# 100 tokens instead of 96 gathered in a product-key expert layer: a third group of four, more gathers in the query, first residuals between the last sums of v

## The chip, the cores and the metric

The kernel runs on one core of one Trainium2 chip. The metric is the device time of one launch in microseconds. A core has TensorE (PE, matmul, with its weight loads shown apart as PEld), VectorE (DVE), ScalarE (ACT), GpSimd (POOL) and SyncE (SP, which here only issues DMAs). 16 DMA engines move the data.

## The reference

One decoder layer on 256 tokens of width 2048, all in float32: attention (eight differential heads, eight stick-breaking heads) and an output projection, then a product-key expert layer (PEER), then a gated embedding, with a layer norm behind each. The part that matters here is PEER, over 16384 experts, of which each token uses 8 heads x 16:

```
q = (xt @ wq).reshape(t, PEER_HEADS, PEER_QDIM)
sa, sb = scores of the two halves of q against 128 keys each
va, ia = lax.top_k(sa, PEER_TOPK)
vb, ib = lax.top_k(sb, PEER_TOPK)
top, sel = lax.top_k(va + vb over all pairs, PEER_TOPK)
eidx = ia * PEER_NKEYS + ib at sel
gates = jax.nn.softmax(top, axis=-1)
act = jax.nn.gelu(einsum('thed,td->the', u[eidx], x))
out = einsum('the,thed->td', gates * act, v[eidx])
```

Then `x = layer_norm(alpha * x + out)`.

## The kernel before

**Two ways through PEER.** Of the 256 tokens the first NSP = 96 are sparse and the other NDT = 160 dense. For the dense tokens all 16384 experts are computed. The first pass (u) has 128 blocks `ia` of 128 experts; a block (`u_block`) loads 1 MB of `peer_u`, multiplies it in 16 matmuls with the 160 columns of `XF`, and ACT writes the Gelu into `A`. f32 matmuls show as two instructions each, so there are 4096. `gate_work` then builds, from one-hot matrices, the gate of each (expert, token) pair (`ps_G`) and multiplies it into `A`, first during the second 64 blocks of u, then during the first 64 blocks of v. The second pass (v) runs twice over the 128 blocks, once for each half of the 2048 outputs, eight matmuls a block (`v_block`, `v_mm`; one load of 1 MB for two blocks).

For the sparse tokens the rows of `peer_u` and `peer_v` that they need are gathered. A group of n tokens (`GROUPS`) puts 128/n copies of its tokens on the 128 partitions, and each copy handles n of the token's 128 experts. So one gather (an indirect DMA on POOL into a tile `gb`, 128 rows of 8 KB, 1 MB) serves 128 pairs of token and expert, and a group of n needs n gathers for u and n for v: 192 in all. DVE uses each: in u (L794) it multiplies `gb` with `xq`, the tokens' rows, and sums; in v (L800) it adds `gb` times a weight `ew` to `y`. `sparse_out` sums the copies with a matmul against a selecting matrix.

**What sets the order.** A planner places the instructions of each engine in the order in which it expects them to be ready; those wrapped in `keep` stay in the order in which they are written. DVE, ACT and POOL work their queue in that order. The DMAs of the weights are issued by SP into five buffers of 1 MB (`wf`).

Gathers are paced: after each block, `gathers(n)` adds n to a running sum, and for each whole number reached one gather is written. It begins with a `mark`, a DMA of four bytes in SP's queue behind the weight loads; POOL copies it (`pace`), and only then issues the gather. So a gather is released when SP has got so far, about five loads ahead of PE. The paces are GQ = 1.3 a block in the query (from the fourth of 16 blocks on), GU = 0.715 in u, GV = 0.3575 in v. There are NGB = 3 buffers `gb` and 32 marks; gather k's use is written behind the issue of gather k+2.

**Top-k work.** The query's 16 blocks make the scores of the 8 heads. After every second one, `topk_work` does one head of the first 128 tokens on DVE and POOL (`topk_heads(0, h, 1)`, `head_slots`), and `place` writes the head's expert numbers into `eig` with small DMAs on POOL. In u each block runs one step: `gates(0)`, the softmax of the first 128 tokens, whose Exp (L702) stands in ACT's queue and waits for a subtraction on DVE (L700); then the 34 steps of `topk_heads(1, 0, 8)`; then `gates(1)` and the transposes for `gate_work`.

**The end of v.** The last STAG = 6 blocks of the second half are loaded ahead (`held`) and summed output by output, so that `v_out` can copy a finished pair of outputs to `yT` while PE sums the next. `res2` transposes `yT` back and adds the residual. `sparse_out` stands after block 113 of the second half, `res2` of the first half of the outputs after blocks 114 and 115, and two loads of `ple_gate` with their splitting (`sg2.parts`) after blocks 116 and 119.

Of the kernel before, what the change touches and what calls it, by code (L numbers as in the profile page):

```python
# [38 lines left out]
SEG1 = 64  # L39
SEG2 = NIA - SEG1  # L40

GROUPS = ((0, 64), (64, 32))
NSP = sum(n for _, n in GROUPS)
NDT = T - NSP
SELB = 8
NGB = 3

GQ = 1.3
GU = 0.715
GV = 0.3575  # L50
GSCALE = 2.0 ** 15
GB = 5
OHB = 5
# [102 lines left out]
def build(tc, a, out):  # L156
# [496 lines left out]
        yield from ()  # L653

    keep = tc.keep_in_program_order

    def topk_heads(t, h0, n):

# [38 lines left out]
    def gates(t):  # L697

        g = gate[:, t]
        keep(nc.vector.tensor_tensor(g, CV[:, t], CV[:, t, :, 0:1].to_broadcast([P, PH, TOPK]),  # L700
                                     op=ALU.subtract))
        keep(nc.scalar.activation(g, g, AF.Exp))  # L702
# [17 lines left out]
        place(0, slice(h, h + 1), 0)  # L720

    def place(i, hs, w):
        t0, n = GROUPS[i]
        m = n // PH
        dst = eig[i].rearrange("p w (h m) -> p w h m", h=PH)
        for q in range(P // n):
            nc.gpsimd.dma_start(dst[q * n:(q + 1) * n, w, hs],
                                eg[t0:t0 + n, w, hs, q * m:(q + 1) * m])

    def topk_work():  # L730
        nc.vector.tensor_copy(io128, io128f)
        for h in range(PH):
            for _ in topk_heads(0, h, 1):
                pass
            head_slots(h)
            yield
        for i in range(1, len(GROUPS)):
            place(i, slice(0, PH), 0)
# [31 lines left out]
    def sparse_work():  # L770

        xq = []
        for i, (t0, n) in enumerate(GROUPS):
            xq.append(gin.tile([P, D], F32, name=f"xq{i}", tag=f"xq{i}"))
            for q in range(P // n):
                nc.gpsimd.dma_start(xq[i][q * n:(q + 1) * n, :], a["s_x1"][t0:t0 + n, :])
        made = []

        dots, acts = [], []

        def advance():

            if acts:
                i, b = acts.pop(0)
                keep(nc.vector.tensor_tensor(ew[i][:, b], ew[i][:, b],
                                             eig[i][:, 1, b].bitcast(F32), op=ALU.mult))
            if dots:
                i, b = dots.pop(0)
                keep(nc.scalar.activation(ew[i][:, b], eact[i][:, b], AF.Gelu_apprx_tanh))
                acts.append((i, b))  # L790

        def use(kind, i, j, g):
            if kind == "u_rows":
                keep(nc.vector.scalar_tensor_tensor(g, g, 1.0, xq[i], op0=ALU.mult, op1=ALU.mult,  # L794
                                                    accum_out=eact[i][:, j:j + 1]))
            elif j == 0:
                ys[i] = gin.tile([P, D], F32, name=f"y{i}", tag=f"xq{i}")
                keep(nc.vector.tensor_scalar(ys[i], g, ew[i][:, j:j + 1], None, op0=ALU.mult))
            else:
                keep(nc.vector.scalar_tensor_tensor(ys[i], g, ew[i][:, j:j + 1], ys[i],  # L800
                                                    op0=ALU.mult, op1=ALU.add))
            if j % SELB == SELB - 1:
                advance()
                if kind == "u_rows":
                    dots.append((i, slice(j + 1 - SELB, j + 1)))

        for kind in ("u_rows", "v_rows"):
            for i, (_, n) in enumerate(GROUPS):
                for j in range(n):

                    mark = gin.tile([1, 1], F32, name="mark", tag="mark", bufs=32)
                    keep(nc.sync.dma_start(mark, a["c_iota"][0:1, 0:1]))
                    keep(nc.gpsimd.tensor_copy(pace, mark))  # L813
                    g = gin.tile([P, D], F32, name="gb", tag="gb", bufs=NGB)
                    keep(nc.gpsimd.indirect_dma_start(  # L815
                        out=g, out_offset=None, in_=a[kind],
                        in_offset=bass.IndirectOffsetOnAxis(ap=eig[i][:, 0, j:j + 1], axis=0)))
                    made.append((kind, i, j, g))
                    if len(made) >= NGB:
                        use(*made.pop(0))  # L820
                    yield
        while made:
            use(*made.pop(0))

    def sparse_out():

        for i, (t0, n) in enumerate(GROUPS):
            per = min(ND, 512 // n)
            for d0 in range(0, ND, per):
                ps = pbank(pp, "ps_y")  # L830
                for j in range(per):
                    keep(nc.tensor.matmul(ps[:, j * n:(j + 1) * n],  # L832
                                          ys[i][:, (d0 + j) * P:(d0 + j + 1) * P], sel[i],
                                          start=True, stop=True))
                nc.scalar.copy(yT[:, d0:d0 + per, t0:t0 + n],  # L835
                               ps[:, :per * n].rearrange("p (j t) -> p j t", j=per))
# [190 lines left out]
    for ia in range(SEG1, NIA - STAG):  # L1027
        v_block(1, ia, psv2, keep if ia >= NIA - STAG - 16 else lambda ins: ins)
        gathers(GV)
        if ia == NIA - STAG - 14:  # L1030
            while not run(sparse, 1):
                pass
        if ia == NIA - STAG - 9:
            sparse_out()
        if ia in (NIA - STAG - 8, NIA - STAG - 7):
            for t in range(NT):
                res2(t, 4 * (ia - NIA + STAG + 8), 4)
        if ia in (NIA - STAG - 6, NIA - STAG - 3):
            sg2.order = keep
            parts0 += list(sg2.parts(a["ple_gate"][0, len(parts0) // 4]))  # L1040
    held = [v_load(1, ia) for ia in range(NIA - STAG, NIA)]
# [224 lines left out]
```

## Time and profile before

| | |
|---|---|
| median of 3 runs | 1825.09 us (1825.09 to 1826.13) |
| profiled execution | 1826.57 us, its span 1824.6 us |
| PE busy | 1786.7 us, 98% |
| DVE busy | 1045.2 us, 57% |
| ACT busy | 544.4 us, 30% |
| POOL busy | 500.6 us, 27% |
| moved by DMA | 599.33 MB, mean 328 GB/s |
| mean granted TensorE clock | 0.995 |

The groups of the profile give a line of the kernel, an engine, an operation, the tile written and those read, the shapes, how often, the busy time in microseconds and the mean of one instruction in ns, then the idle time ahead of it and what ended that. Matmuls overlap, so busy time divided by count is their distance, and the mean of one is longer. A row of stretches has each engine's busy time with the count, then the granted clock, the share of the DMA engines and GB/s. In the timeline a row is a start, a duration and a run of like instructions. Some matmul records are missing. By stages: the query runs from 417 to 533 us, u to 1119, the first half of v to 1415, and the second to 1704.

### The profile page before, as it was taken

The numbers are of one execution on the slowest core, as the hardware profiler recorded it, in microseconds if no ns is written. First come the engines' busy times: TensorE is split into PE (matmuls) and PEld (weight loads), VectorE is DVE, ScalarE is ACT, GpSimd is POOL, SyncE is SP. The second block draws the span as 40 slices with busy tenths as digits, with TensorE's granted clock in tenths as the row PEclk, the third lists the DMA queues.
The fourth block names the chain that finished last, engine by engine and source line by source line (L and its number), as shares of the span: only waits on it lengthen the run. The fifth ranks groups of instructions, "written<-read, shape, count | busy, mean of one in ns | idle before, by whom it ended". The sixth has DMA issues, their size and how long they took to land.

```text
span 1824.6 us, 30303 instructions
## 1 busy us (share of the span) xinstructions
PE 1786.7 (98%) x12094; PEld 1679.9 (92%) x12094; DVE 1045.2 (57%) x1643; ACT 544.4 (30%) x1365; POOL 500.6 (27%) x579
## 2 busy tenths in 40 slices
PE   8999999999999999999999999999999999999896
PEld 6888888888899999999999999999999999999766
DVE  5555588654677894543554544975433333343686
ACT  5677477642010001002333331862000000001532
POOL 0133033006445242322222212222234233220241
PEclk9999999999999999999999999999999999999998
DMA  7554644668789999999999999999999999996561
GB/s 278 187 171 163 231 145 156 231 212 266 306 316 374 420 420 416 395 420 401 415 379 383 380 391 353 420 419 350 421 421 420 415 416 415 419 421 267 212 258 53
DMA packets 98717, 599.33 MB, mean 328 GB/s; under 512 B 13072, under 2 KB 14912, under 8 KB 35600
## 3 DMA queue, kind: packets, MB, share of 16 engines
q1 hardware_dynamic: 66768, 384.24, 54.4%
q0 software_dynamic: 30080, 208.57, 28.5%
q10 hardware_dynamic: 1728, 4.59, 0.7%
q8 instruction: 95, 1.56, 0.3%
q14 instruction: 46, 0.38, 0.1%
HBM read 590.96 MB, written 6.29 MB: 327 GB/s over the span
## 4 chain that ended last, share of the span: by engine, by line
PE 82%; issue 6%; DVE 5%; DMA 4%; POOL 2%; ACT 1%; SPq 0%; DVEq 0%; POOLq 0%; ACTq 0%
PE ps_v L956 30%; PE ps_u L206 23%; PE ps_qk L195 7%; PE ps_qk L197 3%; PE ps_q L206 2%; PE ps_v L214 2%; PE ps_v L215 2%; PE ps_v L213 2%; PE ps_mix L213 1%; PE ps_mix L214 1%; PE ps_mix L215 1%; DMA wf<-peer_u 1%; PE ps_gate L214 1%; PE ps_gate L213 1%; PE ps_gate L215 1%
## 5 line engine op out<-in xcount | busy, mean ns | idle before, releaser
L206 PE MATMUL ps_u<-XF,wf 128*128 128x160 f32 x4096 | 572.4, 301 | 6.8 <-ACT A L906 6.6
L956 PE MATMUL ps_v<-A,wf 128*128 128x160 f32 x4096 | 569.1, 301 | 0.6 <-DVE A L877 0.6
L206 PEld LDWEIGHTS ps_u<-XF,wf 128*128 128x128 f32 x4096 | 560.3, 191 | 9.7 <-ACT A L906 8.8
L956 PEld LDWEIGHTS ps_v<-A,wf 128*128 128x128 f32 x4096 | 558.5, 191 | 1.6 <-DVE A L877 0.7
L800 DVE SCALAR_TENSOR_TENSOR y<-gb,ew,y 128x2048 f32<-128x2048 f32 x94 | 220.9, 2350 | 242.0 <-DMA gb<-v_rows,eig 241.8
L108 DVE TENSOR_TENSOR wl<-wf,wh 128x1024 fp32r<-128x1024 f32 (+1 forms) x201 | 222.7, 1132 | 98.3 <-ACT wh L107 97.0
L794 DVE SCALAR_TENSOR_TENSOR gb<-gb,xq 128x2048 f32<-128x2048 f32 x96 | 218.7, 2286 | 93.3 <-DMA gb<-u_rows,eig 90.5
L107 ACT CAST wh<-wf 128x1024 fp32r<-128x1024 f32 (+1 forms) x201 | 172.8, 889 | 111.7 <-PE ps_qk L195 29.4
L815 POOL DMA_INDIRECT gb<-u_rows,eig x96 | 101.3, 1055 | 334.4 <-DVE gb L794 213.9
L195 PE MATMUL ps_qk<-X,wh 128*128 128x512 f32 x512 | 185.2, 401 | 0.0
L815 POOL DMA_INDIRECT gb<-v_rows,eig x96 | 115.8, 1206 | 196.8 <-DVE y L800 148.8
L906 ACT ACTIVATE A<-ps_u 128x160 f32<-128x160 f32 x128 | 38.5, 303 | 434.7 <-PE ps_u L206 389.4
L813 POOL COPY pace<-mark 1x1 f32<-1x1 f32 x192 | 95.3, 496 | 252.1 <-DMA mark<-c_iota 251.4
L197 PE MATMUL ps_qk<-X,wl 128*128 128x256 f32 x512 | 146.1, 285 | 0.0
L859 ACT ACTIVATE hi<-eq,ghf 128x64 f16<-128x64 f16 x320 | 107.3, 335 | 52.5 <-DVE eq L853 48.5
L195 PEld LDWEIGHTS ps_qk<-X,wh 128*128 128x128 f32 x512 | 96.6, 189 | 21.9 <-issue 1.0
L206 PE MATMUL ps_q<-XF,wf 128*128 128x256 f32 x512 | 113.5, 380 | 0.0
L853 DVE TENSOR_TENSOR eq<-io,iaT 128x320 f16<-128x320 f16 x64 | 31.2, 488 | 133.8 <-ACT lo L860 133.8
L206 PEld LDWEIGHTS ps_q<-XF,wf 128*128 128x128 f32 x512 | 96.2, 191 | 12.0
L860 ACT ACTIVATE lo<-eq,glf 128x64 f16<-128x64 f16 x320 | 107.0, 334 | 0.0
L197 PEld LDWEIGHTS ps_qk<-X,wl 128*128 128x128 f32 x512 | 96.4, 188 | 2.5 <-issue 1.3
L835 ACT COPY XF<-ps_y 128x512 f32<-128x512 f32 x3 | 1.8, 585 | 253.2 <-PE ps_y L832 253.2
(232 smaller groups left out, 1791.2 us busy)
## 6 DMA issues: line engine op xcount, KB each, us to landing
wf<-peer_u SPq DMA_DIRECT2D x128, 1024.0 KB
wf<-peer_v SPq DMA_DIRECT2D x128, 1024.0 KB
wf<-w_qk SPq DMA_DIRECT2D x64, 512.0 KB
wf<-w_out SPq DMA_DIRECT2D x32, 512.0 KB
wf<-peer_wq SPq DMA_DIRECT2D x16, 1024.0 KB
wf<-ple_gate SPq DMA_DIRECT2D x16, 1024.0 KB
wf<-w_v SPq DMA_DIRECT2D x31, 512.0 KB
mark<-c_iota SPq DMA_DIRECT2D x192, 0.0 KB
```

Of the source, the lines that this page charges most:

```text
L107: self.order(nc.scalar.copy(wh, src))
L108: self.order(nc.vector.tensor_tensor(wl, src, wh.bitcast(F32), op=ALU.subtract))
L195: nc.tensor.matmul(ps, wh[:, j * P:(j + 1) * P], xt[:, dt, :], start=dt == 0, stop=False)
L197: nc.tensor.matmul(ps[:, :T], wl[:, j * P:(j + 1) * P], xt[:, dt, :T], start=False, stop=dt == ND - 1)
L206: nc.tensor.matmul(ps[:, :T - t0], wf[:, dt * P:(dt + 1) * P], xt[:, dt, t0:], start=dt == 0, stop=dt == ND - 1)
L794: keep(nc.vector.scalar_tensor_tensor(g, g, 1.0, xq[i], op0=ALU.mult, op1=ALU.mult, accum_out=eact[i][:, j:j + 1]))
L800: keep(nc.vector.scalar_tensor_tensor(ys[i], g, ew[i][:, j:j + 1], ys[i], op0=ALU.mult, op1=ALU.add))
L813: keep(nc.gpsimd.tensor_copy(pace, mark))
L815: keep(nc.gpsimd.indirect_dma_start(out=g, out_offset=None, in_=a[kind], in_offset=bass.IndirectOffsetOnAxis(ap=eig[i][:, 0, j:j + 1], axi ...
L859: nc.scalar.mul(hi[:, j, :], eq[:, j, :], ghf[:, t])
L860: nc.scalar.mul(lo[:, j, :], eq[:, j, :], glf[:, t])
L956: return nc.tensor.matmul(ps[:, (j % 2) * NDT:(j % 2 + 1) * NDT], vf[:, j * P:(j + 1) * P], W_of(ia), start=False, stop=ia == NIA - 1 and ...
```

## The change

- A third group of four tokens: 100 are sparse and 156 dense. It needs four gathers for u and four for v, 200 in all. Its tokens stand on the partitions in 32 copies, so its part of `xq` comes in 32 DMAs of 32 KB on POOL, and `place` writes its expert numbers and gates in 32 small DMAs on SP instead of POOL, once both are known.
- Paces: GQ 2.0, GU 0.695, GV 0.3475. So 26 gathers are marked in the query, and v's last one after block 116 of the second half.
- `gates(0)` comes after five of the 16 selections of the second 128 tokens; after eight further steps follows the third group's `place`. The gates are multiplied into `ew` only once they are there (`gated`).
- `sparse_out` stands behind the last loads of v, directly ahead of the last sums; `res2` of the first outputs moves between the last sums; the loads of `ple_gate` come after blocks 113 and 117.

```
-GROUPS = ((0, 64), (64, 32))
+GROUPS = ((0, 64), (64, 32), (96, 4))
-GQ = 1.3
-GU = 0.715
-GV = 0.3575
+GQ = 2.0
+GU = 0.695
+GV = 0.3475
...
+    gated = []
...
-            for i in range(len(GROUPS)):
-                place(i, slice(0, PH), 1)
+            for i, (_, n) in enumerate(GROUPS):
+                if n >= PH:
+                    place(i, slice(0, PH), 1)
+            gated.append(t)
...
     def place(i, hs, w):
         t0, n = GROUPS[i]
+        if n < PH:
+            for q in range(P // n):
+                nc.sync.dma_start(eig[i][q * n:(q + 1) * n],
+                                  eg[t0:t0 + n, :, q // TOPK::PH // n, q % TOPK])
+            return
...
+        second = topk_heads(1, 0, PH)
+        for _ in range(5):
+            next(second)
+            yield
         yield from gates(0)
-        yield from topk_heads(1, 0, PH)
+        for _ in range(8):
+            next(second)
+            yield
+        for i, (_, n) in enumerate(GROUPS):
+            if n < PH:
+                place(i, slice(0, PH), slice(0, 2))
+        yield from second
         yield from gates(1)
...
-            if acts:
+            if acts and gated:
...
-            if j % SELB == SELB - 1:
+            if j % SELB == SELB - 1 or j == GROUPS[i][1] - 1:
                 advance()
                 if kind == "u_rows":
-                    dots.append((i, slice(j + 1 - SELB, j + 1)))
+                    dots.append((i, slice(j - j % SELB, j + 1)))
...
-        if ia == NIA - STAG - 14:
+        if ia in (NIA - STAG - 9, NIA - STAG - 5):
+            sg2.order = keep
+            parts0 += list(sg2.parts(a["ple_gate"][0, len(parts0) // 4]))
+        if ia == NIA - STAG - 3:
             while not run(sparse, 1):
                 pass
-        if ia == NIA - STAG - 9:
-            sparse_out()
-        if ia in (NIA - STAG - 8, NIA - STAG - 7):
-            for t in range(NT):
-                res2(t, 4 * (ia - NIA + STAG + 8), 4)
-        if ia in (NIA - STAG - 6, NIA - STAG - 3):
-            sg2.order = keep
-            parts0 += list(sg2.parts(a["ple_gate"][0, len(parts0) // 4]))
     held = [v_load(1, ia) for ia in range(NIA - STAG, NIA)]
-    for b in range(4):
+    sparse_out()
+
+    between = [(), ((0, 4),), (), ((4, 4), (8, 2)), (), ((10, 2),), (), ((12, 2),)]
+    for j in range(8):
+        for d0, nd in between[j]:
+            for t in range(NT):
+                res2(t, d0, nd)
         for ia in range(NIA - STAG, NIA):
-            for j in (2 * b, 2 * b + 1):
-                v_mm(psv2[b], j, ia, held[ia - NIA + STAG])
-        v_out(1, b, psv2[b])
-        if b < 3:
-            for t in range(NT):
-                res2(t, 8 + 2 * b, 2)
+            keep(v_mm(psv2[j // 2], j, ia, held[ia - NIA + STAG]))
+        if j % 2:
+            v_out(1, j // 2, psv2[j // 2])
```

More of the change, by code (lines that the diff above doesn't have):

```diff
@@ L737, in topk_work @@
         for i in range(1, len(GROUPS)):
-            place(i, slice(0, PH), 0)
-        yield from gates(0)
-        yield from topk_heads(1, 0, PH)
+            if GROUPS[i][1] >= PH:
+                place(i, slice(0, PH), 0)
+        second = topk_heads(1, 0, PH)
+        for _ in range(5):
+            next(second)
+            yield
+        yield from gates(0)
+        for _ in range(8):
[5 more added lines that the diff above has]
+        yield from second
         yield from gates(1)
@@ L1029, in build @@
         gathers(GV)
-        if ia == NIA - STAG - 14:
+        if ia in (NIA - STAG - 9, NIA - STAG - 5):
+            sg2.order = keep
+            parts0 += list(sg2.parts(a["ple_gate"][0, len(parts0) // 4]))
+        if ia == NIA - STAG - 3:
             while not run(sparse, 1):
                 pass
-        if ia == NIA - STAG - 9:
-            sparse_out()
-        if ia in (NIA - STAG - 8, NIA - STAG - 7):
-            for t in range(NT):
-                res2(t, 4 * (ia - NIA + STAG + 8), 4)
-        if ia in (NIA - STAG - 6, NIA - STAG - 3):
-            sg2.order = keep
-            parts0 += list(sg2.parts(a["ple_gate"][0, len(parts0) // 4]))
-    held = [v_load(1, ia) for ia in range(NIA - STAG, NIA)]
-    for b in range(4):
-        for ia in range(NIA - STAG, NIA):
-            for j in (2 * b, 2 * b + 1):
-                v_mm(psv2[b], j, ia, held[ia - NIA + STAG])
-        v_out(1, b, psv2[b])
-        if b < 3:
-            for t in range(NT):
-                res2(t, 8 + 2 * b, 2)
+    held = [v_load(1, ia) for ia in range(NIA - STAG, NIA)]
+    sparse_out()
+    between = [(), ((0, 4),), (), ((4, 4), (8, 2)), (), ((10, 2),), (), ((12, 2),)]
+    for j in range(8):
+        for d0, nd in between[j]:
+            for t in range(NT):
+                res2(t, d0, nd)
+        for ia in range(NIA - STAG, NIA):
+            keep(v_mm(psv2[j // 2], j, ia, held[ia - NIA + STAG]))
+        if j % 2:
+            v_out(1, j // 2, psv2[j // 2])
     stats2 = []
```

## The prediction

> **What bounds the kernel now.** I read first the page's busy times, then the groups by shape, then stretches of the span stage by stage, then the order of single instructions where PE stands.
>
> ```profile
> PE 1786.7 (98%) x12094; PEld 1679.9 (92%) x12094; DVE 1045.2 (57%) x1643; ACT 544.4 (30%) x1365; POOL 500.6 (27%) x579
> L206 PE MATMUL ps_u<-XF,wf 128*128 128x160 f32 x4096 | 572.4, 301 | 6.8 <-ACT A L906 6.6 <-DMA wf<-peer_u 0.2
> L956 PE MATMUL ps_v<-A,wf 128*128 128x160 f32 x4096 | 569.1, 301 | 0.6 <-DVE A L877 0.6
> ```
>
> PE is the bound: 98% busy, and 8192 of its instructions are the two dense passes over the experts, one column for each of the 160 dense tokens. Next, the stretches: the query, three parts of the first pass (u), the part in which the gate matrices are also built, and the second half of v.
>
> ```profile
> core 0: us, PE busy (x) PEld busy (x) DVE busy (x) ACT busy (x) POOL busy (x), PEclk, DMA share, GB/s
> 417.00:533.00 116.00, 116.00 (x570) 103.21 (x569) 72.43 (x236) 14.08 (x36) 60.76 (x71) 1.00 0.80 288
> 561.00:640.00 79.00, 75.83 (x544) 75.59 (x544) 63.61 (x183) 7.73 (x24) 26.13 (x43) 0.98 1.00 403
> 640.00:665.00 25.00, 23.05 (x161) 22.02 (x162) 24.17 (x64) 1.61 (x6) 4.57 (x8) 1.00 1.01 421
> 820.00:1270.00 450.00, 449.15 (x3724) 443.57 (x3725) 254.85 (x306) 175.07 (x712) 101.77 (x138) 1.00 0.97 390
> 1270.00:1640.00 370.00, 370.00 (x2721) 369.52 (x2720) 143.14 (x62) 1.70 (x4) 115.39 (x125) 1.00 1.01 417
> ```
>
> Transfers are the second bound, and close: 421 GB/s is the most any stretch shows, v runs at 417, and only the query (288) has room. Where transfers are full, PE can lose:
>
> ```profile
> 645.01 4.59 PE L206 MATMUL ps_u<-XF,wf 128*128 128x160 f32 x32 [0.39 <-ACT A L906]
> 649.99 4.59 PE L206 MATMUL ps_u<-XF,wf 128*128 128x160 f32 x32 [0.38 <-ACT A L906]
> 649.64 0.30 ACT L906 ACTIVATE A<-ps_u 128x160 f32<-128x160 f32 x1 [4.58 <-PE ps_u L206]
> ```
>
> These u blocks start 4.98 us apart. ACT, named as the releaser, itself waits for PE (third row); 1.0486 MB of weights in 4.98 us is 211 GB/s, half of 421. So while gathers are behind and always have something queued, they take half of the transfers, the weights get the other half, and PE waits for weights. How far gathers are behind when u begins:
>
> ```profile
> L812 SPq DMA_DIRECT2D mark<-c_iota x19: 228/277/307, 416.0 to 519.8; - x19
> L815 POOL DMA_INDIRECT gb<-u_rows,eig x11: 957/1024/1220, 460.5 to 522.6; - x11
> ```
>
> Up to 533 us, 19 marks were released and 11 gathers issued: eight behind. The pace is not what holds gathers in the query.
>
> **The change, part by part.** *Four dense tokens fewer.* The price of a column comes from two lengths of the same kind of instruction:
>
> ```profile
> 443.56 7.07 PE L206 MATMUL ps_q<-XF,wf 128*128 128x256 f32 x32
> 450.91 7.07 PE L206 MATMUL ps_q<-XF,wf 128*128 128x256 f32 x32
> 1275.97 386.85 PE ps_v L956 x2848
> 1662.66 7.23 PE L832 MATMUL ps_y<-sel,y 128*128 128x64 f32 x64
> ```
>
> The first two rows are two queries, 7.35 us apart. 256 columns follow each other at (7.07 - 0.38)/31 = 215.8 ns (0.38 is the duration of one), 160 columns at 386.85/2848 = 135.8 ns: 0.833 ns a column. Four columns save 3.33 ns, over 8192 instructions **-27.3 us**. The last row (64 and 32 columns, (7.23 - 0.27)/63 = 110.5 ns) shows a floor, but 156 columns (132.5 ns) lie above it.
>
> ```profile
> L868 PE MATMUL ps_G<-lo,ohb 128*128 128x64 f16 x320 | 33.5, 194 | 0.1
> L867 PE MATMUL ps_G<-hi,ohb 128*128 128x64 f16 x320 | 31.8, 193 | 0.1
> ```
>
> The gate matrices lose four tokens of 160, that is 16 of these 640 products at 102 ns: **-1.6 us**. The third group adds 32 selecting products in sparse_out (16 of f32, two passes each) at the 110.5 ns floor: **+3.5 us**. PE's own sum is -25.4 us.
>
> *Eight gathers more, nine more of them meant for the query* (26 instead of 16.9). A gather moves 1.0486 MB, 2.49 us at 421 GB/s. What the query can take is set by DVE, not by transfers:
>
> ```profile
> 430.00:562.00 132.00, 130.65 (x706) 118.97 (x704) 92.52 (x309) 14.91 (x37) 61.09 (x74) 1.00 0.85 310
> L794 DVE SCALAR_TENSOR_TENSOR gb<-gb,xq 128x2048 f32<-128x2048 f32 x14 | 31.6, 2284 | 16.7 <-DMA gb<-u_rows,eig 13.9 <-DMA eig<-eg 2.8
> 439.10 2.98 POOL L776 DMA_DIRECT2D xq<-s_x  x6 [5.07 <-DVE TIf L671]
> 460.46 1.04 POOL L815 DMA_INDIRECT gb<-u_rows,eig  x1 [12.51 <-DMA mark<-c_iota]
> ```
>
> From 430 to 562 DVE does the eight heads of the first 128 tokens and 14 uses of gathers. Without the uses (31.6) it is 60.9 us, 7.6 us a head. With four gathers a head instead of two or three, a head costs 7.6 + 4 x 2.28 = 16.7 us of DVE against 14.7 us for two queries, before any of the 16.7 us of waits. So DVE becomes the bound of the query. The 32 new pieces of xq stand on POOL ahead of the first gather: 32 x 0.50 = 16 us, of which 442 to 458 lies in the time in which POOL waited anyway until 460.5; bounds 0 and +16, I take 4, nearest to that row. From 464 to 533, at 17 to 21 us a head, come 13 to 16 gathers; I take 14. Marks then stand at 26 + 4 x 0.695, some 28: 14 behind instead of 8. Six more gathers have to be caught up in u, where transfers are full: 6 x 2.49 = **+15 us**. The bounds are 0 (all of it in the stretch 820 to 1270, which at 390 of 421 GB/s has room for 13 gathers) and +22 (all nine).
>
> The Trainium skill, page "DMA: Bandwidth & Descriptors", section "Bandwidth", says that between HBM and SBUF the HBM side binds, at about 358 GB/s. The 370 us at 417 GB/s above are over that, so here the row decides; by the page's figure the six gathers would cost 17.6 us and the sum would be 2.7 us worse. The same section gives 0.95 us to a transfer of 64 KB and calls smaller ones bound by descriptors; the new xq pieces are 32 KB, and by that figure, an estimate, 32 of them one after another would take 30 us instead of 16 and cost some three gathers of the query more.
>
> *Moved and new waits.* gates(0) comes five steps later. Its Exp stands in ACT's queue ahead of the next Gelu:
>
> ```profile
> ACT gate L702 <- DVE gate L700: 16.8, 1, 16.8
> 543.30 0.30 ACT L906 ACTIVATE A<-ps_u 128x160 f32<-128x160 f32 x1 [2.72 <-PE ps_u L206]
> 543.72 1.28 ACT L702 ACT_TABLE_LOAD   x1
> 561.50 0.28 DVE L700 TENSOR_TENSOR gate<-CV 128x128 f32<-128x128 f32 x1
> 563.79 0.40 PE L206 MATMUL ps_u<-XF,wf 128*128 128x160 f32 x1 [3.14 <-ACT A L906]
> ```
>
> Already before, ACT waits 16.8 us in it for DVE, the four banks of ps_u fill behind it, and PE stands for 3.1 us. In the new order 27 uses stand before it instead of 14, and five more selections. I put no change here into the forecast: Exp's turn and DVE's work both move back, by 21 us (five blocks of 4.24) and by more than that; the rest is the first rival.
>
> The third group's indices go by 32 DMAs on SP, ahead of weight loads.
>
> ```profile
> 519.85 0.28 SPq L812 DMA_DIRECT2D mark<-c_iota  x1
> 1628.08 0.34 SPq L97 DMA_DIRECT2D wf<-peer_v  x1
> ```
>
> At 0.28 us each, 9 us of SP's queue; five loads in flight (five blocks, 21 us) cover it if DVE has written eg by then, eight blocks after the gates. Without that cover the weights are late by DVE's delay and the 9 us.
>
> *The tail.* Marks end at ia 116 instead of 105 of the last half, sparse_out comes after ia 121 instead of 113.
>
> ```profile
> 1634.91 0.96 POOL L815 DMA_INDIRECT gb<-v_rows,eig  x1 [0.16 <-issue]
> 1650.45 2.35 DVE L800 SCALAR_TENSOR_TENSOR y<-gb,ew,y 128x2048 f32<-128x2048 f32 x1 [3.90 <-DMA gb<-v_rows,eig]
> ```
>
> The last use ends at 1652.8, sparse_out starts at 1662.66: 9.9 us of room. The distance from the last mark to sparse_out shrinks by three blocks of 2.12 us, so 3.5 us of room are left. Two loads of ple_gate now come before the end of the gathers (up to 5 us at 2.49 each). Bounds 0 and +5; I take 0, because weights and gathers already share the transfers half and half. The first residuals move between the last sums: the same transposes and the same DVE work, only later, so +-0.5 us, nothing. DVE's 8 more uses in v (2.35 us each) lie in its idle time: 143 of 370 us busy.
>
> **The sum.** -27.3 - 1.6 + 3.5 + 15 = -10.4 us. The profiled execution took 1826.57 us (span 1824.6), the median of the runs is 1825.09, so the profile is 1.5 us high: 1826.6 - 10.4 = 1816.2 profiled, **1815 us** as a median.
>
> **The rivals.**
>
> *PE stands at gates(0)* (slower). DVE reached the gates' subtraction at 561.5. Thirteen more uses are 13 x 2.28 = 30 us, and five selections of 128 keys 5 x 1.67 = 8 us by the first and the last of one's eight instructions:
>
> ```profile
> 430.32 0.29 DVE L631 MAX8 TV<-S 128x8 f32<-128x128 f32 x1 [10.66 <-ACT S L652]
> 431.71 0.28 DVE L636 FIND_INDEX8 TI<-TV,s 128x8 uint32<-128x128 f32 x1
> ```
>
> That puts the subtraction at 600. If ACT keeps Exp just five blocks later, ACT blocks from 545 + 21 = 566, PE has used up its four banks at 582 and stands 18 to 20 us instead of 3; the DMAs on SP wait for the same write. Part is given back, since transfers go on in that time and catch up gathers: net +12 to +20 on the forecast, 1827 to 1835, with 1830 as its value. It decides once DVE is more than four blocks (17 us) later than Exp's turn. For it speaks the 16.8 us wait of before; against it, that before Exp stood behind the Gelu of the second block (the row at 543.30) though it is written after the first, so the planner of the order moves it back when it expects DVE late. Chance 0.30.
>
> *The query takes all nine.* DVE's waits for gathers (16.7 us) disappear because four are in work at a time; nothing is left to catch up: -25.4, 1800; with a part of it, 1800 to 1809. Against it: 16.7 us of work a head for 14.7 us. Chance 0.12.
>
> *Gathers late at sparse_out.* PE waits there for y; 3.5 us of room are gone when v's gathers run 8 to 13 us later than now: +5 to +9, 1820 to 1824. For it: v at 417 of 421 GB/s, and shorter blocks ask for 0.8475 x 1.0486 MB in 2.12 us, 419. Chance 0.10.
>
> *156 columns cost what 160 cost* (rows no longer start at multiples of 64 bytes). No row shows such a step; then nothing is gained: 1842. Chance 0.03.
>
> **How the numbers follow.** The forecast, 1809 to 1822 by the bounds of the gathers' term, has 0.45. What this kernel's measurement can tell from no change is 0.2%, 3.65 us: faster is below 1821.4, slower above 1828.7. Faster: the forecast's case but for a little, the second rival, and about half of the third: 0.55. Slower: the fourth, most of the first, and a little of stalls that add up: 0.30. Same: the rest, 0.15. The range leaves out half of the second rival at the low end and the fourth and the worst of the first at the high end: 1806 to 1836; the forecast's own is 1809 to 1822.
>
> **What would show it.** The two large groups at 128x156, v blocks 2.12 us apart instead of 2.17: the columns. 13 to 16 gathers issued by 533 and 28 marks: the term of +15; more blocks of u at 4.98 us between 600 and 800 than before. The wait of ACT's Exp for DVE and PE's longest wait for ps_u: the first rival, above 10 us it wins. PE idle ahead of ps_y in sparse_out: the third. The forecast is wrong if gathers by 533 are over 20 or PE stands over 10 us at the start of u.

## The result: 48 us slower

The changed kernel takes 1873.32 us (median of 6 runs, 1871.13 to 1877.48), the kernel before in the same runs 1825.09 us: a ratio of 1.0266, 95% interval 1.025 to 1.0282. The forecast of 1815 us (1806 to 1836) is wrong in sign, and the time lies 37 us above the range. The profiled execution took 1875.39 us, span 1873.6 us.

The page of the changed kernel, busy times and the two large groups:

```profile
PE 1788.1 (95%) x12110; PEld 1673.0 (89%) x12110; DVE 1059.8 (57%) x1656; ACT 541.3 (29%) x1351; POOL 541.3 (29%) x628
L206 PE MATMUL ps_u<-XF,wf 128*128 128x156 f32 x4096 | 561.2, 299 | 28.6 <-DMA wf<-peer_u 26.0
L977 PE MATMUL ps_v<-A,wf 128*128 128x156 f32 x4096 | 559.4, 299 | 11.4 <-DVE A L898 7.4
```

The columns came as forecast: both groups are shorter. But PE now idles 28.6 us in u, 26.0 of them for weights (6.8 us before, nearly all behind ACT), and 11.4 us in v, 7.4 of them for DVE. In a part of v in which PE does not pause, its timeline gives the distance:

```profile
1312.77 301.20 PE L977 MATMUL ps_v<-A,wf 128*128 128x156 f32 x2272
```

(301.20 - 0.3)/2271 = 132.5 ns instead of 135.8. So about 27 us were won, and 76 lost. Where, by stages: each entry is worked out from the trace, as the distance between starts of matmuls, for "gap" from the last matmul of u to the first of v. Lag is marks released less gathers issued at the last matmul of u. The versions named e and f are the experiments.

| kernel | median us | u, first 32 blocks | rest of u | lag | gap | v, 240 blocks | end of v |
|---|---|---|---|---|---|---|---|
| before | 1825.1 | 148.4 | 433.6 | 7 | 3.3 | 538.9 | 44.4 |
| after | 1873.3 | 164.3 | 427.6 | 16 | 35.1 | 531.9 | 58.6 |
| e1 spread | 1874.4 | 166.3 | 425.2 | 16 | 32.9 | 533.5 | 58.2 |
| e2 paces of before | 1853.2 | 155.1 | 426.3 | 10 | 7.9 | 536.8 | 66.3 |
| e3 two groups | 1833.5 | 145.6 | 435.4 | 8 | 8.7 | 539.3 | 48.2 |
| e4 tail of before | 1872.0 | 162.3 | 428.1 | 16 | 34.0 | 530.8 | 57.0 |
| e5 slots in 3 DMAs | 1867.2 | 139.2 | 431.7 | 20 | 47.7 | 532.1 | 56.8 |
| e6 xq in 1 DMA | 1855.0 | 163.9 | 426.5 | 11 | 15.9 | 532.5 | 58.7 |
| e7 both | 1850.1 | 149.8 | 426.7 | 13 | 24.3 | 531.4 | 59.5 |
| e8 both, paces of before | 1853.6 | 157.5 | 427.2 | 10 | 11.3 | 537.0 | 66.5 |
| e9 e7, 8 gathers left out | 1826.8 | 146.8 | 426.2 | 8 | 9.0 | 533.4 | 56.3 |
| e10 e7, sums split | 1841.7 | 149.7 | 427.2 | 13 | 26.9 | 535.9 | 46.1 |
| e11 e7, no marks late in u | 1852.0 | 148.7 | 426.3 | 2 | 13.6 | 546.1 | 59.5 |
| e12 e10, slots placed later | 1837.1 | 146.2 | 426.9 | 13 | 23.5 | 536.4 | 48.6 |
| f1 before, order of gates | 1833.0 | 141.7 | 436.8 | 8 | 3.8 | 545.7 | 47.7 |
| f2 before, new paces | 1839.9 | 153.9 | 436.2 | 8 | 8.7 | 538.8 | 44.4 |
| f3 e12, middle paces | 1855.8 | 156.8 | 428.5 | 11 | 13.3 | 544.5 | 56.1 |

Against before: +15.9, -6.0, +31.8, -7.0 and +14.2 us, together the 49 us of the spans. Three places carry it.

*The start of u.* The queue of SP, and PE behind it:

```profile
580.84 71.50 SPq L97 DMA_DIRECT2D wf<-peer_u  x16
652.44 26.49 SPq L731 DMA_DIRECT2D eig<-eg  x32
679.03 3.94 SPq L833 DMA_DIRECT2D mark<-c_iota  x11
```

```profile
691.19 9.05 PE L206 MATMUL ps_u<-XF,wf 128*128 128x156 f32 x49 [18.00 <-DMA wf<-peer_u]
```

The 32 placing DMAs take SP 0.83 us each: 0.64 us of issue, as a rule, and some pauses. No weight load is issued among them, and 11 marks, which the gathers need, stand behind them and behind 16 loads.

*The gap between u and v.* Stretches (the gap is the second row), and DVE's groups in the gap:

```profile
core 0: us, PE busy (x) PEld busy (x) DVE busy (x) ACT busy (x) POOL busy (x), PEclk, DMA share, GB/s
534.00:698.00 164.00, 141.53 (x1028) 140.09 (x1028) 109.78 (x278) 13.07 (x39) 55.07 (x76) 0.93 0.93 370
1125.00:1161.00 36.00, 15.92 (x97) 9.19 (x96) 30.05 (x36) 20.35 (x86) 20.50 (x20) 0.61 0.86 304
1161.00:1453.00 292.00, 289.33 (x2371) 286.86 (x2371) 166.78 (x149) 78.05 (x316) 90.08 (x100) 0.99 1.00 406
1453.00:1693.00 240.00, 238.47 (x1796) 237.76 (x1796) 88.42 (x39) 0.31 (x1) 67.91 (x78) 1.00 1.01 419
```

```profile
L821 DVE SCALAR_TENSOR_TENSOR y<-gb,ew,y 128x2048 f32<-128x2048 f32 x7 | 16.4, 2345 | 2.6 <-DMA gb<-v_rows,eig 2.6
L815 DVE SCALAR_TENSOR_TENSOR gb<-gb,xq 128x2048 f32<-128x2048 f32 x2 | 4.6, 2281 | 0.0
L898 DVE SCALAR_TENSOR_TENSOR A<-ps_G,A 128x320 f32<-128x320 f32 (+1 forms) x10 | 4.4, 461 | 0.0
L876 DVE TENSOR_TENSOR ohb<-io,ibT 128x640 f16<-128x640 f16 (+1 forms) x6 | 4.4, 727 | 0.0
```

In the gap DVE is busy for 30 of 36 us and PE works for 16, much of it at half clock (0.61). v can't start until A1 is scaled by the gate matrices (L898), and on DVE these steps stand, in program order, among the uses of the gathers. Gathers that are behind at the end of u are therefore worked off here, with PE waiting, and so are the gate steps that are behind: at the last matmul of u 22 of A1's 32 scalings are done, before it was 31. Twice in u DVE itself waited for ACT, the reverse of my first rival:

```profile
645.50 0.29 DVE L705 TENSOR_REDUCE gs<-gate 128x8 f32<-128x128 f32 x1 [16.27 <-ACT gate L703]
763.12 0.28 DVE L701 TENSOR_TENSOR gate<-CV 128x128 f32<-128x128 f32 x1
800.50 0.29 DVE L705 TENSOR_REDUCE gs<-gate 128x8 f32<-128x128 f32 x1 [37.10 <-ACT gate L703]
```

The first row is gates(0), the other two gates(1). The Exps stand in ACT's order after 24 and 55 Gelus of u, where they stood after 2 and 40 before: the planner expected DVE later than it came. The gathers pay for it: in the shorter wait none is issued (624.9 to 651.0 us), in the longer one (763.5 to 803.8 us) the lag rises from 10 (763 us) to 15 (803 us). In between it had even fallen to 0 (36 marks, 36 gathers at 673 us), but only because SP released no mark from 577 to 679 us. The first one-hot matrix of gate_work is made at 893.8 us, before at 820.0.

*The end of v.* The sums of sparse_out by shape:

```profile
L853 PE MATMUL ps_y<-sel,y 128*128 128x4 f32 x32 | 7.0, 354 | 0.0
L853 PE MATMUL ps_y<-sel,y 128*128 128x32 f32 x32 | 5.4, 339 | 0.0
L853 PE MATMUL ps_y<-sel,y 128*128 128x64 f32 x32 | 3.7, 273 | 0.0
```

The same 32 passes take 3.7, then 5.4, then 7.0 us, although the columns get fewer: 5.2 us after their start, at 1723.3 us, the granted clock goes to half, for 13.7 us, and their distance from 110 to 213 ns. sparse_out takes 15.3 us instead of 7.0. That is 8.3 of the 14.2 us at the end of v; the rest is a wait of 2.5 us for weights ahead of it and 6.8 us at half clock around it.

And in the query, which the table leaves out, the first gather is late (POOL):

```profile
L797 POOL DMA_DIRECT2D xq<-s_x x38 | 19.1, 505 | 26.0 <-DMA xq<-s_x 20.9 <-DVE TIf L672 4.7 <-issue 0.2
484.13 1.12 POOL L836 DMA_INDIRECT gb<-u_rows,eig  x1 [0.17 <-issue]
```

The 38 pieces cost 19.1 us of POOL and 20.9 us of waits for earlier ones: in the trace these DMAs take eight semaphores in turn, and each piece from the ninth on waits for the one eight before it to land. The first gather goes out at 484.1 us instead of 460.5, and by 533 us there are 28 marks and 12 gathers.

### The profile page after: what moved, and what is told of

It reads as the page before. It is cut to its first block, busy times and chain, and to the rows that moved or that the text cites. A ratio compares the mean times of both kernels' runs of the same rounds, so it can differ in the third digit from the quotient of the medians.

```text
span 1873.6 us, 30491 instructions
## 1 busy us (share of the span) xinstructions
PE 1788.1 (95%) x12110; PEld 1673.0 (89%) x12110; DVE 1059.8 (57%) x1656; ACT 541.3 (29%) x1351; POOL 541.3 (29%) x628
## 4 chain that ended last, share of the span: by engine, by line
PE 74%; DMA 12%; issue 7%; DVE 3%; POOL 2%; ACT 1%; SPq 1%; DVEq 0%; POOLq 0%; ACTq 0%
PE ps_v L977 26%; PE ps_u L206 16%; DMA wf<-peer_u 7%; PE ps_qk L195 6%; PE ps_q L206 6%; PE ps_qk L197 3%; DMA wf<-peer_v 3%; PE ps_v L215 2%; PE ps_v L214 2%; PE ps_mix L213 2%; PE ps_v L213 1%; PE ps_mix L214 1%; PE ps_mix L215 1%; DMA gb<-v_rows,eig 1%; POOL gb L836 1%
## 5 line engine op out<-in xcount | busy, mean ns | idle before, releaser
L206 PE MATMUL ps_u<-XF,wf 128*128 128x156 f32 x4096 | 561.2, 299 | 28.6 <-DMA wf<-peer_u 26.0
L206 PEld LDWEIGHTS ps_u<-XF,wf 128*128 128x128 f32 x4096 | 549.4, 191 | 33.4 <-issue 24.0
L977 PE MATMUL ps_v<-A,wf 128*128 128x156 f32 x4096 | 559.4, 299 | 11.4 <-DVE A L898 7.4
L977 PEld LDWEIGHTS ps_v<-A,wf 128*128 128x128 f32 x4096 | 550.6, 192 | 13.4 <-DVE A L898 7.6
L821 DVE SCALAR_TENSOR_TENSOR y<-gb,ew,y 128x2048 f32<-128x2048 f32 x97 | 228.0, 2351 | 240.9 <-DMA gb<-v_rows,eig 240.8
L815 DVE SCALAR_TENSOR_TENSOR gb<-gb,xq 128x2048 f32<-128x2048 f32 x100 | 229.8, 2300 | 93.1 <-DMA gb<-u_rows,eig 92.9
L834 POOL COPY pace<-mark 1x1 f32<-1x1 f32 x200 | 107.1, 535 | 285.1 <-DMA mark<-c_iota 284.0
L927 ACT ACTIVATE A<-ps_u 128x156 f32<-128x156 f32 x128 | 38.5, 301 | 475.6 <-PE ps_u L206 442.8
L836 POOL DMA_INDIRECT gb<-v_rows,eig x100 | 123.0, 1230 | 133.7 <-DVE y L821 81.7
L214 PE MATMUL ps_gate<-wl,X 128*128 128x512 f32 (+1 forms) x144 | 53.8, 375 | 4.7 <-DVE wl L108 4.6
```

What stands on the lines that cost most here:

```text
L206: nc.tensor.matmul(ps[:, :T - t0], wf[:, dt * P:(dt + 1) * P], xt[:, dt, t0:], start=dt == 0, stop=dt == ND - 1)
L214: nc.tensor.matmul(ps, hi, wl, start=False, stop=False)
L836: keep(nc.gpsimd.indirect_dma_start(out=g, out_offset=None, in_=a[kind], in_offset=bass.IndirectOffsetOnAxis(ap=eig[i][:, 0, j:j + 1], axi ...
L977: return nc.tensor.matmul(ps[:, (j % 2) * NDT:(j % 2 + 1) * NDT], vf[:, j * P:(j + 1) * P], W_of(ia), start=False, stop=ia == NIA - 1 and ...
```

## The experiments

Theory S: SP's row starves PE, a loss of its own. Theory L: what counts is how many gathers are behind when u ends. Theory X: the pieces of xq on POOL make that lag. Theory B: transfers are full, so a gather costs its 2.49 us wherever it stands.

**e1, the 32 DMAs spread, two to a step**

```
-                place(i, slice(0, PH), slice(0, 2))
+                for _ in place_small(i):
+                    next(second, None)
+                    yield
```

> The changed kernel, with the third group's 32 placing DMAs issued two to a step of the top-k work instead of all in one step, so that marks and weight loads stand between them on SP. Theory S (the stall at SP is a loss of its own): SP's 26.5 us of one row go, PE's idle of 18.0 us before block 32 and the slow blocks behind it go, and nothing later gives it back: 1848 to 1855 us. Theory L (what sets the time is DVE's list of gathers, which has to be worked off before v): PE reaches the end of u some 20 us sooner and waits there as much longer, the gap between the last sum of u and the first of v grows from 39.7 us to about 60: 1868 to 1874 us.

1874.4 us: no change, but not for L's reason, since u is no shorter. SP's queue:

```profile
648.27 1.50 SPq L741 DMA_DIRECT2D eig<-eg  x2
649.81 0.42 SPq L841 DMA_DIRECT2D mark<-c_iota  x1
...
681.68 2.69 SPq L741 DMA_DIRECT2D eig<-eg  x4
684.47 0.35 SPq L841 DMA_DIRECT2D mark<-c_iota  x1
684.92 0.36 SPq L97 DMA_DIRECT2D wf<-peer_u  x1
```

The planner put marks among them but no load: from 648.2 to 684.9 us there is none. So this version is not what it was to test, and decides nothing.

**e2, the paces of before** (GQ, GU, GV 1.3, 0.715, 0.3575)

> The changed kernel with the three paces of before (1.3, 0.715, 0.3575). Theory L (nine more gathers written into the query stand ahead of the gates on DVE, and with the first gather at 484 us they are a lag of 17 that is paid at the end of u): Exp of the gates stands after 10 and 42 Gelus instead of 24 and 55, DVE's waits of 16 and 37 us for it shrink, marks less gathers is 8 to 10 at 533 us and 6 to 8 at the end of u, and the gap before v falls from 39.7 to 10 to 18 us: 1845 to 1855 us. Theory S: the 32 DMAs still stand in one row of SP, so their stall of about 22 us stays, and the gap with it: 1868 to 1876 us.

1853.2 us, 20 less, as L expected. The Exps stand after 10 and 42 Gelus, DVE's waits for them are 0 and 18.9 us, the lag falls to 10 (L said 6 to 8) and the gap to 7.9 us (L: 10 to 18); u's start gains 9 us as well. The end of v loses 7.7: the paces spread 198 of 200 gathers, the last use of y ends at 1700.9 us, and PE stands 9.25 us in sparse_out until then.

**e3, two groups**, all else of the change kept

> The changed kernel with two groups, 96 tokens gathered and 160 columns, all else as changed (paces, order of the gates, tail). The columns cost 27.3 us more, the placing DMAs on SP, the 32 further copies of x rows on POOL, 8 gathers and the third group's share of sparse_out (about 8 us) are gone. Theory S (third group carries the loss): 1873 + 27 - 22 - 8 less what the start of the gathers 20 us sooner gives: 1845 to 1865 us, near before. Theory L (the paces carry it): gap before v stays over 25 us and the total is 1865 to 1885 us.

1833.5 us, ratio to before 1.0044 (1.0024 to 1.0065). That is below the ranges of both theories, and on S's side: the third group carries 40 of the 48 us although it saves 27 us of columns. With the same 28 marks, the first gather goes out at 459.5, and the lag at the end of u is 8. The paces alone do not make the lag.

**e4, the end of v as before**

> The changed kernel with the end of v as it was before: gathers done 14 blocks ahead of the held loads, sparse_out and the first residuals among the blocks, the weights of the gate where they were. Theory T (sparse_out behind all of v's blocks but the held ones runs 15.5 us instead of 7, its small matmuls bring the clock to half, and the loads of the gate stand ahead of v's): 8 to 12 us less, 1861 to 1866 us. Rival (the third group's columns cost the same wherever sparse_out stands, and an earlier end of the gathers adds a wait for y): no change, 1870 to 1876 us.

1872.0 us: the end of v gains 1.6 us, and the total is the rival's, not T's. sparse_out takes 18.7 us there, 3.1 of them a wait for the third group's y; still in one stretch, it is no shorter for standing earlier.

**e5, the slots in three DMAs** over a small tensor in DRAM

```
-            for q in range(P // n):
-                nc.sync.dma_start(eig[i][q * n:(q + 1) * n], ...)
+            nc.sync.dma_start(a["s_eg"], eg[t0:t0 + n].rearrange("t w h k -> t w (h k)"))
+            for v in range(2):
+                nc.sync.dma_start(eig[i][:, v],
+                                  a["s_eg"][:, v].rearrange("t (q j) -> q t j", j=n))
```

> The changed kernel with the third group's slots placed by three DMAs (100 tokens' last four rows of eg to DRAM as one piece, read back as two) in place of 32. In the spread version no load of peer_u stood between the 32 DMAs either, so it took nothing away; this one takes the row of 26.5 us on SP away. Theory S (that row starves PE): the first 32 blocks of u take 140 to 146 us instead of 164, and the total is 1848 to 1856 us if the gap before v stays at 35 us. Theory L (PE has to wait for DVE's gathers before v in any case): the gap grows by what u gains, 1868 to 1875 us.

```profile
534.00:673.00 139.00, 136.93 (x1028) 136.08 (x1027) 83.42 (x201) 13.23 (x38) 46.57 (x62) 1.00 1.01 405
1105.00:1153.00 48.00, 18.04 (x124) 10.32 (x124) 44.81 (x54) 28.06 (x116) 29.57 (x27) 0.56 0.83 305
```

Both theories are right in part. The first row: 32 blocks in 139 us, 25 less than after, so S's stall was real. The second: the gap grows from 35 to 48 us with a lag of 20, and DVE is busy in 44.8 of them. Of 25 us, 6 are left in the total (1867.2, just under L's range).

**e6, xq of the third group in one DMA**

```
+                nc.gpsimd.dma_start(xq[i], a["s_x1"][None, t0:t0 + n, :].to_broadcast([P // n, n, D]))
```

> The changed kernel with the third group's x rows brought by one DMA that reads the four rows 32 times, in place of 32 DMAs on POOL; the 32 placing DMAs on SP stay. Theory X (the 32 issues on POOL hold the first gather from 460 to 484 us and make the lag): first gather at 460 to 464 us, 17 gathers issued at 533 us, lag at the end of u 6 to 10 instead of 16, gap before v 5 to 12 us, total 1843 to 1852 us with the stall at SP still there. Theory L2 (the 26 marks of the query, not the start, make the lag): gap over 25 us, 1866 to 1874 us.

```profile
L797 POOL DMA_DIRECT2D xq<-s_x x1: 597/597/597, 442.0 to 442.0; - x1
467.09 1.04 POOL L839 DMA_INDIRECT gb<-u_rows,eig  x1 [17.40 <-DMA eig<-eg]
```

First gather at 467.1, 15 by the start of u, lag 11, gap 15.9 us, 1855.0 us, with the stall at SP still there. Each number misses X's range by a little, and the gap and the total are far from L2's: most of the lag is X's, not all.

**e7, both repairs**

> The changed kernel with both: one DMA for the third group's x rows, three for its slots. If the two are what the third group costs, its 4 columns less a pass pay: the two-group version's 1833.5 us less 27 us of columns, plus 8 gathers at up to 2.5 us and 8 us of sparse_out: 1818 to 1836 us. If something else of the third group costs as much (its 8 gathers, the gathers' order on DVE): over 1845 us.

1850.1 us, 23 less than after, but over 1845, and beyond the 1836 that two causes would leave at most: the third group has a third cost. With its early start (465.3 us) e7 issues 16 gathers by 533 us, the upper end of the prediction's 13 to 16: DVE's pace was read rightly there, the start was not.

**e8, both repairs and the paces of before**

> As the version with both, and with the three paces of before. If the paces of the change are a loss of their own (nine more gathers ahead of the gates on DVE): 5 to 15 us under the version with both. If they were a loss only because the gathers began late: within 5 us of it, or over it, since some 2 to 3 gathers are then left for the end of v (the spread of the paces gives 198 of 200).

1853.6 us. The gap gives 13 us; u's start takes back 8, v 6 and the end of v 7. With the early first gather the slower paces are no gain.

**e9, e7 without the eight gathers**

```
-            for i, (_, n) in enumerate(GROUPS):
+            for i, (_, n) in enumerate(GROUPS[:2]):
-GU, GV = 0.695, 0.3475
+GU, GV = 0.663, 0.3315
```

> The version with both repairs, with the third group's 8 gathers and their 8 uses left out (4 tokens' sparse part is then wrong: the sums of the second group stand in for theirs) and the paces scaled to 192 gathers (0.663, 0.3315). Everything else of the third group stays. Theory L (each gather that has not been done at the end of u costs about 3.4 us before v, by the gap of 3.3 us at a lag of 7 and 47.7 at 20): 4 fewer marks by the end of u, lag 9 instead of 13, gap 8 to 14 us instead of 24, total 1832 to 1842 us. Rival (the DMA engines are full from u to the end, and each gather costs its 2.49 us wherever it stands): the same 8 times 2.49, 20 us less, 1828 to 1832 us. Rival (the gap comes from ps_G and the scaling alone): under 4 us less, 1846 to 1850 us.

1826.8 us: 23.3 less, 2.9 us a gather; more than L expected in all (8 to 18) and a little more than B (20). Lag 8 and gap 9.0 us are as L expected; PE's wait for A1 is down to one short row (below). Stage by stage B does not hold here: the gap gives 15.3 us, with 2 gathers issued in it instead of 7, but v's 240 blocks are 2.0 us longer with four gathers fewer. And the gathers are not all that went: the paces differ too, the Exp of gates(1) stands after 43 Gelus instead of 51, and DVE does not wait for it, where it waits 30.4 us in e7. So the 23 us are the price of eight gathers with what hangs on them in this order.

```profile
PE ps_v L981 <- DVE A L902: 2.9, 1, 2.9
```

**e10, sparse_out in three pieces**, the first group's 20 blocks and the second's 2 blocks ahead of the held loads

> The version with both repairs, with sparse_out cut in three: the first group's sums 20 blocks and the second's 2 blocks ahead of the held ones, the third's last. Theory T2 (15 us of small matmuls in one stretch bring the granted clock to half, at 1708.6 to 1722.3 us in the version with both): sparse_out's stretch at the end shrinks to 2 to 4 us, no half clock there, blocks 250 and 252 back to under 3.5 us, total 6 to 10 us less: 1840 to 1844 us. Rival (the clock halves by the share of work in a longer window, or PE waits for the last y anyway): under 3 us less.

```profile
1650.59 3.68 PE L857 MATMUL ps_y<-sel,y 128*128 128x64 f32 x32
...
1692.78 3.65 PE L857 MATMUL ps_y<-sel,y 128*128 128x32 f32 x32
...
1698.47 3.94 PE L857 MATMUL ps_y<-sel,y 128*128 128x4 f32 x32
```

1841.7 us, 8.3 less, as expected: the three pieces take 3.7, 3.7 and 3.9 us, where e7's one stretch takes 15.2. The granted clock in the same 20 us, e10 and then e7:

```profile
1690.00:1710.00 20.00, 20.00 (x153) 20.00 (x152) 2.62 (x8) 1.22 (x3) 0.00 (x0) 0.91 0.58 224
1690.00:1710.00 20.00, 20.00 (x125) 20.00 (x125) 0.00 (x0) 1.97 (x4) 0.00 (x0) 0.70 0.52 206
```

At half clock are 3.4 us (1701.6 to 1705.1) instead of 13.7 (1698.0 to 1711.7), so it isn't gone as T2 said. e4, which moved the stretch whole, gained 1.3 us, so its length counts, not its place. Not all of the 8.3 us are that: e7's wait of 3.4 us for weights ahead of the sums (1673.7 us) is gone too.

**e11, no marks in the last 16 blocks of u**, GV 0.392

> The version with both repairs, with no gathers written into the last 16 blocks of u and a pace of 0.392 in v, which brings those 11 back. Theory L alone (the lag at the end of u is what counts): lag 2 to 4, gap 3 to 6 us instead of 24, total 1828 to 1835 us. Theory B (the DMA engines carry 420 GB/s in v already, so each gather that moves into v lengthens it by 2.49 us): gap 3 to 6 us, v longer by 15 to 27 us, total 1845 to 1857 us.

1852.0 us: the total is B's. 11 marks are moved, but by the end of u as many gathers are issued as in e7 (104); what moves are the 7 that e7 issues in the gap, 6 of them into the 240 blocks. These grow by 14.7 us, 2.45 us a gather, B's price; the gap gives 10.7, 1.5 a gather. L alone is out; also, with no gather in the gap it is still 13.6 us (both theories said 3 to 6), so some of it is the gate matrices' own work on DVE and ACT: 25 of A1's 32 scalings are done at the end of u, as in e7.

**e12, e10 with the slots placed behind gates(1)**

> The version with the split sparse_out, and the third group's three placing DMAs written behind the second gates, so that fewer marks and weight loads stand behind a DMA that waits for DVE. If SP's wait for DVE (6.4 us, and 5.1 us for the way through DRAM, with blocks 24 and 25 of u at 8.7 and 7.2 us) is what keeps u's first 32 blocks at 149.8 us: 140 to 145 us there, 4 to 8 us under the split version in u, of which the gap takes half or more again: 2 to 6 us less in all. If DVE's top-k work sets it: no change.

1837.1 us, 4.7 less, as expected in all: u's start goes from 149.7 to 146.2 (140 to 145 expected) and the gap from 26.9 to 23.5, and the end of v takes back 2.5. This is the best version with a third group; it is still slower than before, ratio 1.0067 (1.0046 to 1.0088).

**f1, before with the gates five steps later; f2, before with the new paces**

```
+        second = topk_heads(1, 0, PH)          # f1
+        for _ in range(5):
+            next(second)
+            yield
         yield from gates(0)
+        yield from second
```

> The kernel before with one part of the change alone: the first gates five steps into the second half's top-k work (and the multiplication by the gates held back until they are written). Theory G (before, Exp stands after 2 Gelus and waits 16.8 us for DVE, which costs PE 5 us at blocks 5 and 6 of u): Exp after 7 Gelus, no block of u over 5.1 us among the first ten, 3 to 5 us less, 1820 to 1823 us. Rival (DMA engines full: what PE gains there it gives back as a longer gap before v): within 1 us of before.

> The kernel before with another part alone: the three paces of the change (2.0, 0.695, 0.3475), two groups, 192 gathers (the multiplication by the gates held back until they are written). If the paces are the 7 us by which the two-group version of the changed kernel stands over before: gap before v 8 to 12 us, 1830 to 1836 us. If with an early first gather they cost nothing, and the 7 us are the end of v (tail 48.2 us against 44.4): 1823 to 1828 us.

f1: 1833.0 us, ratio 1.0043 (1.0029 to 1.0058). Both expectations miss. u's start gains 6.7 us, more than theory G said, but the rest of u loses 3.2, v 6.8 (with PE waiting 5.6 us for a one-hot matrix in its first blocks) and the end 3.3. Where it comes back is seen, why so much does is not isolated. f2: 1839.9 us, ratio 1.0085, above both ranges, though the gap of 8.7 us is as the first said. The gap and u's start each grow by 5 us, and here my first rival stands in the trace, ACT and PE:

```profile
571.50 0.31 ACT L703 ACTIVATE gate<-gate 128x128 f32<-128x128 f32 x1 [21.40 <-DVE gate L701]
573.47 11.77 PE L206 MATMUL ps_u<-XF,wf 128*128 128x160 f32 x68 [8.23 <-ACT A L908]
```

The new paces put more uses ahead of gates(0) on DVE, and with the old order of the gates ACT waits in Exp with the Gelus behind it. Together, with the change's end of v (e3), they cost 8 us, less than the 15 us of the paces alone.

**f3, e12 with paces 1.5, 0.71, 0.36**

> The best version of the third group so far (bulk DMAs, split sparse_out, late placing) with paces between the two (1.5, 0.71, 0.36). Theory B (DMA engines full from 465 us to the last gather; where the marks stand moves time from the gap into v and back): 1834 to 1840 us, as 1837. If the lag at the end of u is a loss of its own: gap 10 to 15 us instead of 23.5, 1824 to 1831 us.

1855.8 us, 19 more than e12; neither expectation. The gap gives 10 us, but Exp comes after 8 Gelus and PE stands 11.8 us behind it, the end of v is 7.5 us longer, and v's 240 blocks, with five more gathers in them, 8 us. It says nothing new on B: another wait took the place of the one removed.

## Why the prediction was wrong, point by point

- *Columns, -27.3 us.* Right: 132.5 ns a matmul, u blocks 4.24 us apart.
- *Six gathers to catch up in u, +15 us.* This step failed, first in its count: I took 4 of 0 to +16 us for the pieces of xq on POOL, and the first gather came 24 us late, so that 12 gathers and not 14 were issued by 533 us. The Trainium skill's estimate in the prediction (page "DMA: Bandwidth & Descriptors", section "Bandwidth": 30 us for 32 pieces one after another) was nearer than my 16 to the 40 us that they took (441.6 to 481.7 us), but what the trace shows is the wait for the piece eight before. The step failed more in its place. I let gathers be caught up in u. They were not: transfers are near full there (391 of 421 GB/s from 700 to 1125 us), DVE stood 16 and 37 us for ACT, and the lag at the end of u is the 16 that it was at 533 us. What was behind was paid ahead of v on DVE, with the gate steps: over the versions the gap grows with the gathers issued in it, from 3.3 us with none (before) over 15.9 with 5 (e6) and 35.1 with 10 (after) to 47.7 with 14 (e5), 2.5 to 3.2 us each. Only a part is the gather's own, 1.5 us by e11. I had the row that says v waits for DVE's scaling (L956, 0.6 us in the prediction's first fence) and read it as a small number instead of as a place where DVE's list is cleared. The price of 2.49 us itself holds where transfers are full: e7's first 32 blocks take 10 us more than e5's with 27 gathers in them instead of 23 (403 and 405 GB/s), and e11's v 2.45 us a gather.
- *32 DMAs on SP, 9 us, covered.* Failed in price and cover: 0.83 us each by the row, 26.5 us, priced from a mark and a load that are single pieces per partition. The cover of five loads is what runs out: PE stands 18 us and starts again at half clock (until 695.9 us). e5 takes 25 us off u's start by removing it; all but 6 were given back, most of them at the gap.
- *sparse_out, +3.5 us.* Mis-sized: +8.3 us, since the distance of 110.5 ns holds only while the clock is full. With the same number of passes in three pieces e10 needs 11.3 us, 4.3 more than before, near the 3.5. (That e10's total is 8.3 us lower as well is chance: half clock behind the sums and a wait for weights are in it.)
- *First rival (PE behind Exp).* It did not happen in the changed kernel: the planner put Exp late enough that DVE waited for it. My sign for it, PE standing over 10 us at the start of u, did come, but for weights (18.0 us). It is real elsewhere: 8.2 us in f2, 11.8 in f3. *Gathers late at sparse_out* did not happen either (the last use of y ends at 1712.1, the sums start at 1718.1), but does in e2. *156 columns cost 160*: out.
- *Eight more gathers.* With what hangs on them they are worth 23 us (e9), most of the 29 us that four tokens fewer give. I counted only the six of them that would be late, and not the two resources that both sides of the trade use up. With DVE's order and the transfers as they are, a third group of four gains some 5 us at best, before its other DMAs and sums.

The sum of the steps, in the order in which they were undone: 48 us = 23 (both sets of DMAs, e7) + 8 (sparse_out in pieces, e10) + 5 (where the slots are placed, e12) + 12 that e12 still has over before. These 12 hold the 29 us won and the 23 of the eight gathers, so some 18 of other losses: up to 8 for the order of the gates, the paces and the end of v (e3), 4 for the third group's sums. What stays open: the other 6, and how much of the 8 each of the three has once the third group is there.

## What to carry to other kernels

When two resources are both nearly full, price a trade between them on both sides and at the place where the backlog is cleared: here a gather cost about 2.5 us where transfers were full, and up to 3.2 us, with the gate steps beside it, at the point that needs DVE's list to be empty. Price a DMA by its own shape, not by the queue's usual row, and count what is queued behind it: one DMA that repeats its source did the work of 32 and was worth 18 us. An order planned ahead holds engines in both directions, so a late plan stalls the engine that is early.

## What the hardware showed that I had not expected

- A DMA on SP with 4 partitions of 8 scattered 4-byte elements took 0.64 us of the queue (26.49/32 = 0.83 with the pauses), one of 4-byte marks 0.22 to 0.35 us, one of 1 MB 0.33 to 0.38 us.
- TensorE's granted clock went to half while PE issued without a pause, 5.2 us after the start of f32 matmuls with 64 columns and fewer (110, then 213 ns apart; 5.5 us in e7, 8.3 in e9). Stretches of 7.0 us of them passed at full clock (before, f2), and of three pieces of 3.7 to 3.9 us only the last met 3.4 us of half clock (e10). The Trainium skill, page "TensorE: Matmul & The Clock Gate", part 1 on the HAM clock gate, says that the clock follows how busy PE has been and falls to half after an idle window of about 3.4 us. Here there was no idle window, only small matmuls: the measurement goes further than the rule, and what the gate counts stays open.
- 32 small DMAs on POOL held up the first gather by 24 us (20.9 us in 16 waits), where one DMA that repeats its source was issued in 0.6 us. The waits are those of eight semaphores taken in turn, so they show how long a piece takes to land when eight are under way, not a limit of the queue.
